# Down projection of a two-layer diffusion trunk: low parts of the operands moved from GpSimd to VectorE, raw granules three to five loaded ahead of the last store, and the post-norm sums taken one step later

## The chip, the cores and the metric

The kernel runs on one core of one Trainium2 chip. The metric is the device time of one execution in microseconds (us). The time before is the median of three runs. One further execution was recorded by the hardware profiler; every duration below comes from that one.

## The reference, cut to what matters

Two layers of a trunk over 1024 latent tokens, model width 1024, with 256 context tokens beside them. Each layer has a mixer and a gated feed-forward block; the change is in the last product of that block.

```python
def conv_ffn(h, w_up, conv_w, conv_b, w_down):
    u = h @ w_up
    u = lax.conv_general_dilated(u, ...) + conv_b      # width 3, over positions
    a, g = jnp.split(u, 2, axis=-1)
    return (jax.nn.silu(g) * a) @ w_down               # D_FF = 2816 -> 1024

x = x + g2 * rms_norm(conv_ffn(h_lat, ...), norm_post_ffn[l])
if with_ctx_out:                                       # layer 0 only
    ctx = ctx + g2c * rms_norm(conv_ffn(h_ctx, ...), norm_post_ffn[l])
```

All of it is in 32-bit floats, and the output is the latent stream after the second layer.

## The kernel before, in words

**The arithmetic.** TensorE multiplies the type called fp32r. To keep 32-bit accuracy each operand is split in two tiles: a high part (`d_Ah`, `d_Bh`; a cast on ScalarE, L1442) and a low part (`d_Al`, `d_Bl`; raw minus high, L1443, on VectorE or GpSimd, whichever `lo_engine` names). Each product is three matmuls: high by high, high by low of B, low of A by high.

**The down projection** (`ffn_down`) is a Strassen-like product with seven partial products, taken in the order P1, P5, P2, P3, P6, P4, P7. The contraction is cut in six *granules* per product (the sixth is half as wide), numbered 0 to 41 through the seven products (P1 is 0 to 5, P3 18 to 23, P6 24 to 29, P4 30 to 35, P7 36 to 41). A full granule is 24 matmuls of 128x128 by 512 columns. In P7 the last three granules are worked together, row block by row block, so that the four accumulators end one after the other. In layer 0 the context tokens follow as 22 more granules (42 to 63) of 12 matmuls each; layer 1 has none. A is the activation, read back from the DRAM tensor `actd`; B is the weight `w_down`. S and T (`d_s`, `d_t`) are kept sums of blocks, made by VectorE at L1447.

**Order.** In this stretch the instructions of TensorE, ScalarE, VectorE, GpSimd and, from the last step of the up projection on, of SyncE's queue stand in the order in which the program writes them. Each engine works strictly in that order. At step g the loop issues the products of granule g, then `prepare(g + 2)`: the splits (`prep`) of the granule two ahead (five ahead in the context part) and the loads that come after it, then whatever `todo` holds for that step. Operand tiles rotate over three places (six in the context part), so the splits of granule g wait until TensorE has finished granule g - 3. Raw tiles of B rotate over three buffers `w_raw`, those of A over four places `x_B22..`; `first_raws` names other places for the first few granules, tiles of the up projection that are no longer read.

**The start.** `ffn_down` is a generator that the last step of the up projection advances by `next(down, None)`: first the loads of granule 0, then its splits with the loads of 1 and 2, then the splits of 1 and 2. The store of the last activation tile to `actd` (L1262) waits for that step's last VectorE product. The loads of granules 3 and 4 follow it on SyncE's queue. The main loop then calls `loads(4)` once more, so granule 4 is loaded a second time, and `prep(4)` reads that second copy.

**Around the products.** `todo` holds the sums into `y` (L1569), squares on ScalarE (L1566), `scale` (L305, L110 on VectorE, then a power on GpSimd, L111), and `leave`: two scalings (L1591), two additions (L1569) on VectorE and a store issued from GpSimd's queue (L1595, L1597). Keys 0 to 3 are the latent rows whose sums end early; 4 to 7 end in P7; 8 and 9 are the context rows.

Of the kernel before, what the change touches and what calls it, by code (L numbers as in the profile page):

```python
# [50 lines left out]
class Trunk:  # L51
# [1136 lines left out]
    def ffn_up(self, l, src, ctx, x_src, x_dst, hp, pp, tp, es):  # L1188


        nc, a = self.nc, self.a
        raws, W, S, st = {}, {}, {}, {}
# [6 lines left out]
        def part(j, name):  # L1199
            if name[0] == "S":  # L1200
                return S[j, name]
            return raws[j, int(name[1]) - 1][:, 512 * (int(name[2]) - 1):512 * int(name[2])]

        def total(j, name, x, op, y):
            if j < FK:
                t = S[j, name] = sp.tile([P, 512], F32, name="w_s", bufs=3)
                nc.gpsimd.tensor_tensor(out=t, in0=part(j, x), in1=part(j, y), op=op)
# [9 lines left out]
        def product(ps, ws, x, start, stop):  # L1217

            jobs = [(W[w], k) for w in ws for k in range(4)]
            for i, ((wh, wl), k) in enumerate(jobs):  # L1220
                h, lo = wh[:, k * P:(k + 1) * P], wl[:, k * P:(k + 1) * P]
                xhk, xlk = X[x][i]
                self.mm(ps, h, xhk, start and i == 0, False)
                self.mm(ps, h, xlk, False, False)
                self.mm(ps, lo, xhk, False, stop and i == len(jobs) - 1)
# [50 lines left out]
        with self.in_order(*self.compute), ExitStack() as loads:  # L1276
# [4 lines left out]
            early = [lambda: split(0, "A11"), lambda: split(0, "A12")] + [lambda: split(0, "A21")] * ctx + [lambda: split(0, "A22")]  # L1281
# [24 lines left out]
            down = iter(())  # L1306
            for j in range(FK):
                n = j + 1
                if n == FK:
                    loads.enter_context(self.in_order(mybir.EngineType.SP))  # L1310
                    down = self.ffn_down(l, ctx, x_src, x_dst, hp, sp, pp, tp)
# [48 lines left out]
                if j == 0:  # L1360
                    next(sums)
                product(V[:, :512], ("A22",), "T4", True, True)
                total(n, "S3", "A11", OP.subtract, "A21")
                split(n, "S3")
                total(n, "S4", "A12", OP.subtract, "S2")
# [20 lines left out]
    def ffn_down(self, l, ctx, x_src, x_dst, hp, sp, pp, tp, beside=None):  # L1386
# [5 lines left out]
        nc, a = self.nc, self.a  # L1392
# [3 lines left out]
        NG = (H + 1) // 2  # L1396
        width = lambda c: min(2, H - 2 * c)

        def tile(pool, tag, name, n=1024, dtype=F32, bufs=1):
            return pool.tile([P, n], dtype, name=name, tag=tag, bufs=bufs)  # L1400
# [2 lines left out]
        s_home = [(hp, "x_T3" + x) for x in ("0h", "0l", "1h", "1l")] + [(hp, "x_T11l"), (self.wp, "w_A11l")]  # L1403
        t_home = [(hp, "n_t22")] * 2 + [(hp, "x_T1" + x) for x in ("0h", "0l", "1h")] + [(self.wp, "w_A11h")]

        first_raws = {(1, "A"): "x_T30h", (2, "A"): "x_T30l", (2, "B"): "x_T31h", (3, "A"): "x_T31l"}
        S, T, raws, opnd, count = {}, {}, {}, {}, {"A": 0, "B": 0}

        def load(dst, view, n):
# [29 lines left out]
        def split(side, slot, src, n, lo_engine):  # L1439
            tags = more[slot] if slot in more else [homes[slot % 3] + ("0" if side == "A" else "1") + x for x in "hl"]  # L1440
            hi, lo = (tile(hp, t, "d_" + side + x, dtype=F32R) for t, x in zip(tags, "hl"))
            nc.scalar.copy(hi[:, :n], src[:, :n])  # L1442
            lo_engine.tensor_tensor(out=lo[:, :n], in0=src[:, :n], in1=hi[:, :n].bitcast(F32), op=OP.subtract)  # L1443
            return hi, lo
# [35 lines left out]
        def prep(g):  # L1480
            if g >= NS + NC:
                return
            if g >= NS:
                k = g - NS
                opnd[g, "B"] = split("B", g, raws.pop((g, "B")), 1024, nc.gpsimd if k % 2 else nc.vector)
                if k % 4 == 0:
                    opnd[g, "A"] = split("A", k // 4, raws.pop((g, "A")), 256 * min(4, FK - k), nc.vector)
                return
            p, c = order[g // NG], g % NG
            n = 512 * width(c)  # L1490
            ra, rb = raws.pop((g, "A"), None), raws.pop((g, "B"), None)
            if p == "P7":
                total(T[c], rb, OP.subtract, T[c], n)
            elif p == "P4":
                total(rb, rb, OP.subtract, T[c], n)
            early = g < 3
            sides = (("A", S[c] if p in ("P5", "P6", "P7") else ra, nc.gpsimd if early else nc.vector),
                     ("B", T[c] if p in ("P5", "P6", "P7") else rb, nc.gpsimd if early or p in ("P3", "P4", "P7") else nc.vector))

            for side, src, engine in sides[::-1] if p in ("P3", "P5") else sides:  # L1500
                if side == "A" and p == "P5":
                    total(S[c], S[c], OP.add, ra, n)
                elif side == "A" and p == "P3":
                    total(ra, ra, OP.subtract, S[c], n)
                opnd[g, side] = split(side, g, src, n, engine)
            if p == "P1":
                after = lambda: total(T[c], T[c], OP.subtract, rb, n)
                if early:
                    return after
                after()  # L1510
            elif p == "P2":
                total(S[c], S[c], OP.subtract, raws.pop((g, "A2")), n)
            elif p == "P3":
                total(T[c], rb, OP.subtract, T[c], n)
            elif p == "P4":
                total(S[c], raws.pop((g, "A2")), OP.subtract, S[c], n)
# [45 lines left out]
        def at(g, f):  # L1562
            todo.setdefault(g, []).append(f)

        def square(src, ms, h):
            nc.scalar.activation(junk, src, AF.Square, scale=1.0 / 32.0, accum_out=ms[:, h:h + 1])  # L1566
# [18 lines left out]
        def scale(key, ms):  # L1585
            st["r", key] = self.y_rstd(ms)
# [15 lines left out]
        loads(1)  # L1602
        loads(2)
        yield
        after.append(prep(1))
        yield
        after.append(prep(2))
# [14 lines left out]
        y1b = [tile(p, "w_" + t, "y", 512) for p, t in ((self.wp, "A22h"), (self.wp, "A22l"), (sp, "S3h"), (sp, "S3l"))]  # L1622
        y2 = [tile(hp, "x_T4" + x, "y") for x in ("0h", "0l", "1h", "1l")]
        ms1, ms2 = ([self.small.tile([P, 2], F32, name=f"y_ms{j}", bufs=4) for _ in range(4)] for j in range(2))
        for i in range(4):
            at(NG + 1 + i, lambda i=i: nc.scalar.copy(p1[i], X[i]))
            at(2 * NG + 1 + i, lambda i=i: add(y2[i][:, 512:], Y[i], p1[i]))
            at(3 * NG + 1 + i, lambda i=i: (nc.scalar.copy(y1a[i], X[i]), square(X[i], ms1[i], 0)))
            at(4 * NG + 1 + i, lambda i=i: add(y1b[i], Y[i], p1[i]))
            at(5 * NG + 1 + i, lambda i=i: add(y1b[i], X[i], y1b[i]))  # L1630
            at(5 * NG + 2 + i, lambda i=i: (square(y1b[i], ms1[i], 1), scale(i, ms1[i])))
            at(6 * NG + 1 + i // 2, lambda i=i: add(y2[i][:, :512], Y[i], p1[i]))
        for i, (g, g1) in enumerate(((25, 33), (26, 35), (36, 38), (37, 39))):
            at(g, lambda i=i: fetch_x(i, i * P))
            at(g1, lambda i=i: leave(i, (y1a[i], y1b[i]), 0, i * P))
        r2 = lambda i: SEQ // 2 + i * P
# [11 lines left out]
        for i in range(5):  # L1648
            g = 6 * NG + (8 if ctx else 4) + gap * i
# [5 lines left out]
                at(g, lambda i=i - 1: leave(4 + i, halves(y2[i]), 0, r2(i), y2[i]))  # L1655
        for i in range(2 if ctx else 0):
            at(NS + NC - 4, lambda i=i: fetch_x(8 + i, SEQ + i * P))
        loads(3)
        loads(4)
        for kind in range(len(gates)):  # L1660
            for h in range(2):
                nc.sync.dma_start(gates[kind][h], self.gated[l, 1, kind][512 * h:512 * h + 512].partition_broadcast(P))
# [494 lines left out]
```

## Time and profile before

| what | value |
|---|---|
| median of three runs | 3511.76 us (3502.54 to 3518.81) |
| the profiled execution, its own time | 3511.39 us |
| its span in the profile | 3509.6 us (1.8 us lie around it) |
| TensorE busy | 3160.5 us, 90% of the span |
| VectorE busy | 2078.7 us, 59% |
| GpSimd busy | 1639.8 us, 47% |
| ScalarE busy | 1486.1 us, 42% |
| down projection of layer 0, first to last matmul | 1728.4 to 2032.8 us |
| down projection of layer 1, first to last matmul | 3257.9 to 3491.1 us |

The shares are means over stages of very different kinds. A matmul's recorded length overlaps that of its neighbours, so TensorE reads as fully busy whenever matmuls follow each other without a gap; what a stage loses is seen by counting its matmuls over its length.

### The profile page before, as it was taken

Reading aid. Unit: us, or ns where it says so; the run is one execution under the profiler, and the core shown is the slowest. Engines: PE = TensorE matmul, PEld = TensorE weight load, DVE = VectorE, ACT = ScalarE, POOL = GpSimd, SP = SyncE. Lnnn points to the kernel's source line nnn. Section 1 sums busy time; section 2 is a strip of 40 time slices with the busy share of each in tenths; the row PEclk is TensorE's granted clock in tenths of the full one; section 3 lists DMA queues with packets and bytes.
Section 4 is the critical chain, followed back from the end, with each engine's and each line's share of the span. In section 5 each row is a group of like instructions: output and inputs, shape, how many; then the busy total and the mean of one; then the engine's idle time right before and its main releaser. Section 6 shows DMA issues by size and latency. Waiting matters only on the chain. (4 is left out here: it accounts for less than half of the span.)

```text
span 3509.6 us, 49014 instructions
## 1 busy us (share of the span) xinstructions
PE 3160.5 (90%) x18364; PEld 2577.2 (73%) x18364; DVE 2078.7 (59%) x3366; ACT 1486.1 (42%) x2619; POOL 1639.8 (47%) x1174
## 2 busy tenths in 40 slices
PE   5989998779997899999999859999998689999997
PEld 2767676568885688888777638789986468888785
DVE  3525666557775744444578752477775564545678
ACT  3223222266664533333334441466674343434332
POOL 1300111187773566666413410577771167777124
PEclk7999999879998899999999979999998799999998
DMA  6533433321113122121466642222215412222755
GB/s 227 164 118 107 136 110 118 104 72 49 43 47 116 39 78 71 67 70 67 145 237 221 228 149 102 88 62 59 69 44 180 138 60 78 85 79 84 264 180 197
DMA packets 204845, 399.26 MB, mean 114 GB/s; under 512 B 24112, under 2 KB 86064, under 8 KB 204608
## 3 DMA queue, kind: packets, MB, share of 16 engines
q1 hardware_dynamic: 198432, 374.64, 32.2%
q0 software_dynamic: 6176, 21.50, 1.6%
q8 instruction: 144, 2.36, 0.3%
q14 instruction: 93, 0.76, 0.1%
HBM read 322.11 MB, written 74.34 MB: 113 GB/s over the span
## 5 line engine op out<-in xcount | busy, mean ns | idle before, releaser
L111 POOL TENSOR_TENSOR rs_r<-rs_e,mhalf 128x1 f32<-128x1 f32 (+3 forms) x106 | 79.6, 751 | 673.8 <-DVE rs_e L110 662.4
L103 PE MATMUL d_ps<-d_Bl,d_Ah 128*128 128x512 f32 x704 | 283.0, 402 | 19.0 <-POOL d_Bl L1443 15.2
L103 PE MATMUL d_ps<-d_Bh,d_Ah 128*128 128x512 f32 x704 | 281.9, 400 | 12.3 <-ACT d_Bh L1442 11.6
L103 PE MATMUL g_ps<-xh,w_hi 128*128 128x512 f32 (+1 forms) x704 | 279.5, 397 | 5.6 <-ACT w_hi L533 4.4
L103 PE MATMUL d_ps<-d_Bh,d_Al 128*128 128x512 f32 x704 | 281.1, 399 | 1.7 <-DVE d_Al L1443 1.7
L896 POOL TENSOR_SCALAR a_p<-a_p,rl 128x1280 f32<-128x1280 f32 (+1 forms) x80 | 240.4, 3010 | 73.4 <-DVE rl L895 65.3
L1857 POOL TENSOR_SCALAR c_p<-c_p,rl 128x640 f32<-128x640 f32 (+1 forms) x128 | 231.2, 1808 | 84.8 <-DVE rl L1856 59.8
L103 PE MATMUL g_ps<-xh,w_lo 128*128 128x512 f32 (+1 forms) x704 | 259.7, 369 | 4.7 <-POOL w_lo L1763 3.5
L103 PE MATMUL g_ps<-xl,w_hi 128*128 128x512 f32 (+1 forms) x704 | 259.8, 369 | 0.0
L1443 POOL TENSOR_TENSOR d_Bl<-d_rawB,d_Bh 128x1024 fp32r<-128x1024 f32 (+1 forms) x41 | 113.7, 2776 | 304.8 <-ACT d_Bh L1442 298.4
L1228 DVE TENSOR_TENSOR f_u<-u_v,f_p 128x512 f32<-128x512 f32 x88 | 60.5, 688 | 196.0 <-PE u_v L103 196.0
L103 PEld LDWEIGHTS d_ps<-d_Bl,d_Ah 128*128 128x128 f32 x704 | 136.0, 193 | 53.5 <-POOL d_Bl L1443 19.7
L918 DVE TENSOR_TENSOR a_pl<-a_pt,a_ph 128x512 fp32r<-128x512 f32 (+1 forms) x200 | 118.8, 603 | 89.3 <-ACT a_ph L917 88.8
L103 PEld LDWEIGHTS d_ps<-d_Bh,d_Ah 128*128 128x128 f32 x704 | 136.4, 194 | 45.7 <-ACT d_Bh L1442 14.9
L103 PEld LDWEIGHTS g_ps<-xh,w_hi 128*128 128x128 f32 x704 | 135.9, 193 | 45.4 <-issue 27.5
L1214 POOL TENSOR_TENSOR w_S4l<-w_s,w_S4h 128x512 fp32r<-128x512 f32 x44 | 57.2, 1301 | 237.4 <-ACT w_S4h L1213 237.4
L103 PEld LDWEIGHTS d_ps<-d_Bh,d_Al 128*128 128x128 f32 x704 | 136.3, 194 | 31.4 <-DVE d_Al L1443 2.9
L103 PEld LDWEIGHTS g_ps<-xh,w_lo 128*128 128x128 f32 x704 | 135.5, 192 | 29.4 <-POOL w_lo L1763 4.3
L103 PE MATMUL g_ps<-w_hi,xh 128*128 128x512 f32 (+1 forms) x400 | 153.7, 385 | 1.1 <-ACT w_hi L467 1.1
L917 ACT CAST a_ph<-a_pt 128x512 fp32r<-128x512 f32 (+1 forms) x200 | 102.9, 519 | 122.0 <-PE a_pt L916 122.0
L103 PE MATMUL g_ps<-w_lo,xh 128*128 128x512 f32 (+1 forms) x400 | 151.5, 379 | 0.8 <-DVE w_lo L468 0.8
L103 PE MATMUL g_ps<-w_hi,xl 128*128 128x512 f32 (+1 forms) x400 | 151.1, 378 | 0.2 <-DVE xl L268 0.2
(458 smaller groups left out, 9874.0 us busy)
## 6 DMA issues: line engine op xcount, KB each, us to landing
m_raw<-in_w_mod SPq DMA_DIRECT2D x96, 512.0 KB
w_raw<-in_w_up SPq DMA_DIRECT2D x88, 512.0 KB
d_rawA<-actd SPq DMA_DIRECT2D x77, 512.0 KB
d_rawB<-in_w_down SPq DMA_DIRECT2D x74, 512.0 KB
actd<-f_t SPq DMA_DIRECT2D x22, 640.0 KB
d_t<-in_w_down SPq DMA_DIRECT2D x22, 512.0 KB
actd<-f_t SPq DMA_DIRECT2D x22, 512.0 KB
d_s<-actd SPq DMA_DIRECT2D x20, 512.0 KB
```

The lines of the kernel that those rows point to most:

```text
L103: return self.nc.tensor.matmul(out, lhsT, rhs, start=start, stop=stop, skip_group_check=True, **k)
L111: nc.gpsimd.tensor_tensor(out=r[:p, :n], in0=e[:p, :n], in1=self.mhalf[:p, :n], op=OP.pow)
L896: nc.gpsimd.tensor_scalar(Pt[:, :nk], Pt[:, :nk], rl, None, op0=OP.mult)
L917: nc.scalar.copy(ph[:, j:j + n], pt[:, :n])
L918: nc.vector.tensor_tensor(out=pl[:, j:j + n], in0=pt[:, :n], in1=ph[:, j:j + n].bitcast(F32), op=OP.subtract)
L1214: nc.gpsimd.tensor_tensor(out=lo, in0=part(j, name), in1=hi.bitcast(F32), op=OP.subtract)
L1228: nc.vector.tensor_tensor(out=out, in0=x, in1=y, op=OP.add)
L1443: lo_engine.tensor_tensor(out=lo[:, :n], in0=src[:, :n], in1=hi[:, :n].bitcast(F32), op=OP.subtract)
L1857: nc.gpsimd.tensor_scalar(Pt[:, :n], Pt[:, :n], rl, None, op0=OP.mult)
```

## The change

Four edits. The step of the up projection advances the generator once more, and the loads of granules 3 and 4 move to that place, ahead of the last store. Raw tiles 3B, 4A, 4B and 5A get places of their own among the operand tiles `x_T4..` of the up projection, which are dead after its product T4. The low part of B in P3, P4, P7 and in every second context granule goes from GpSimd to VectorE, so that GpSimd makes low parts for granules 0 to 2 alone. And `scale` for keys 0 to 3 comes one step after the square it reads, with key 0's `leave` one step later too.

```diff
                 product(V[:, :512], ("A22",), "T4", True, True)
+                next(down, None)
                 total(n, "S3", "A11", OP.subtract, "A21")
...
-        first_raws = {(1, "A"): "x_T30h", (2, "A"): "x_T30l", (2, "B"): "x_T31h", (3, "A"): "x_T31l"}
+        first_raws = {(1, "A"): "x_T30h", (2, "A"): "x_T30l", (2, "B"): "x_T31h", (3, "A"): "x_T31l",
+                      (3, "B"): "x_T40h", (4, "A"): "x_T40l", (4, "B"): "x_T41h", (5, "A"): "x_T41l"}
...
-                opnd[g, "B"] = split("B", g, raws.pop((g, "B")), 1024, nc.gpsimd if k % 2 else nc.vector)
+                opnd[g, "B"] = split("B", g, raws.pop((g, "B")), 1024, nc.vector)
...
-                     ("B", T[c] if p in ("P5", "P6", "P7") else rb, nc.gpsimd if early or p in ("P3", "P4", "P7") else nc.vector))
+                     ("B", T[c] if p in ("P5", "P6", "P7") else rb, nc.gpsimd if early else nc.vector))
...
         loads(1)
         loads(2)
+        yield
+        loads(3)
+        loads(4)
         yield
         after.append(prep(1))
...
-            at(5 * NG + 2 + i, lambda i=i: (square(y1b[i], ms1[i], 1), scale(i, ms1[i])))
+            at(5 * NG + 2 + i, lambda i=i: square(y1b[i], ms1[i], 1))
+            at(5 * NG + 3 + i, lambda i=i: scale(i, ms1[i]))
...
-        for i, (g, g1) in enumerate(((25, 33), (26, 35), (36, 38), (37, 39))):
+        for i, (g, g1) in enumerate(((25, 34), (26, 35), (36, 38), (37, 39))):
...
-        loads(3)
-        loads(4)
         for kind in range(len(gates)):
```

SyncE's queue in layer 0 at the end of the up projection, before (numbers tell tiles of one name apart; 15848 to 15852 are granule 2, `actd_79<-f_t0_15855` is the last store, 15953 to 15957 granule 3, 15959 to 15963 granule 4, first load):

```order
L1410 DMA d_rawB_15848<-in_w_down 128x2x512
L1410 DMA d_rawA_15850<-actd_79 128x2x512
L1410 DMA d_t_15852<-in_w_down 128x2x512
L1262 DMA actd_79<-f_t0_15855 128x1280
L1410 DMA d_rawB_15953<-in_w_down 128x2x512
L1410 DMA d_rawA_15955<-actd_79 128x2x512
L1410 DMA d_t_15957<-in_w_down 128x2x512
L1410 DMA d_rawB_15959<-in_w_down 128x2x512
L1410 DMA d_rawA_15961<-actd_79 128x2x512
L1410 DMA d_t_15963<-in_w_down 128x2x512
L1662 DMA gate0_15925<-gated_75 128x512
```

and in the changed kernel:

```order
L1412 DMA d_rawB_15848<-in_w_down 128x2x512
L1412 DMA d_rawA_15850<-actd_79 128x2x512
L1412 DMA d_t_15852<-in_w_down 128x2x512
L1412 DMA d_rawB_15874<-in_w_down 128x2x512
L1412 DMA d_rawA_15876<-actd_79 128x2x512
L1412 DMA d_t_15878<-in_w_down 128x2x512
L1412 DMA d_rawB_15880<-in_w_down 128x2x512
L1412 DMA d_rawA_15882<-actd_79 128x2x512
L1412 DMA d_t_15884<-in_w_down 128x2x512
L1262 DMA actd_79<-f_t0_15855 128x1280
L1666 DMA gate0_15937<-gated_75 128x512
L1666 DMA gate0_15938<-gated_75 128x512
```

The six transfers of granules 3 and 4 stood behind the store and stand ahead of it now. The second load of granule 4 stands after the four `gate` loads in both.

VectorE in layer 0 around the turn from P4 to P7, before (the half granule 35 with its sums, then key 0's `leave`):

```order
L305 TENSOR_TENSOR yms<-y_ms_15945 128x1
L110 TENSOR_SCALAR rs_e<-yms 128x1
L1569 TENSOR_TENSOR y<-d_ps,y 128x512
L1447 TENSOR_TENSOR d_rawB<-d_rawB,d_t 128x512
L1443 TENSOR_TENSOR d_Al<-d_rawA,d_Ah 128x512
L1447 TENSOR_TENSOR d_s<-d_rawA,d_s 128x512
L305 TENSOR_TENSOR yms<-y_ms_15946 128x1
L110 TENSOR_SCALAR rs_e<-yms 128x1
L1569 TENSOR_TENSOR y<-d_ps,y 128x512
L1591 SCALAR_TENSOR_TENSOR y<-y,rs_r,gate_15925 128x512
L1591 SCALAR_TENSOR_TENSOR y<-y,rs_r,gate_15926 128x512
L1569 TENSOR_TENSOR y<-y,y_x 128x512 x2
```

and in the changed kernel (granule 35, then granule 36, the first of P7):

```order
L1449 TENSOR_TENSOR d_rawB<-d_rawB,d_t 128x512
L1445 TENSOR_TENSOR d_Al<-d_rawA,d_Ah 128x512
L1445 TENSOR_TENSOR d_Bl<-d_rawB,d_Bh 128x512
L1449 TENSOR_TENSOR d_s<-d_rawA,d_s 128x512
L305 TENSOR_TENSOR yms<-y_ms_15957 128x1
L110 TENSOR_SCALAR rs_e<-yms 128x1
L1571 TENSOR_TENSOR y<-d_ps,y 128x512
L1449 TENSOR_TENSOR d_t<-d_rawB,d_t 128x1024
L1445 TENSOR_TENSOR d_Al<-d_s,d_Ah 128x1024
L1445 TENSOR_TENSOR d_Bl<-d_t,d_Bh 128x1024
L305 TENSOR_TENSOR yms<-y_ms_15958 128x1
L110 TENSOR_SCALAR rs_e<-yms 128x1
```

Each granule has a `d_Bl` more on VectorE; the first `yms` stands behind granule 35's splits instead of ahead of them, and granule 36 comes ahead of key 0's `leave` instead of behind it.

GpSimd in layer 0 from P4's last granule on, before:

```order
L111 TENSOR_TENSOR rs_r<-rs_e,mhalf 128x1
L1443 TENSOR_TENSOR d_Bl<-d_rawB,d_Bh 128x512
L111 TENSOR_TENSOR rs_r<-rs_e,mhalf 128x1
L1595 DMA x2d<-y 128x512 x2
L1443 TENSOR_TENSOR d_Bl<-d_t,d_Bh 128x1024
L111 TENSOR_TENSOR rs_r<-rs_e,mhalf 128x1
L1443 TENSOR_TENSOR d_Bl<-d_t,d_Bh 128x1024
```

and in the changed kernel:

```order
L111 TENSOR_TENSOR rs_r<-rs_e,mhalf 128x1 x2
L1597 DMA x2d<-y 128x512 x2
L111 TENSOR_TENSOR rs_r<-rs_e,mhalf 128x1
L1597 DMA x2d<-y 128x512 x2
L111 TENSOR_TENSOR rs_r<-rs_e,mhalf 128x1
```

Only the powers and the stores are left there. TensorE's and ScalarE's order is the same in both kernels.

## Rows read from the trace of the kernel before

**Rows 1.** The stretches of layer 0's down projection, matmuls and weight loads that touch `d_ps` (and others that touch it): P1; P5 and P2; P3; P7; the context granules. Columns: stretch, length, then busy time and number of instructions for PE, PEld, DVE, ACT, then the granted TensorE clock, the DMA share and GB/s.

```profile
1728.40:1768.70 40.30, 34.39 (x132) 26.82 (x132) 0.00 (x0) 0.00 (x0) 0.92 0.81 293
1768.70:1828.50 59.80, 59.80 (x265) 49.51 (x265) 2.73 (x4) 2.31 (x4) 1.00 0.68 227
1828.50:1859.90 31.40, 30.59 (x134) 24.63 (x133) 0.00 (x0) 4.69 (x12) 1.00 0.36 128
1919.90:1962.60 42.70, 35.35 (x133) 26.99 (x132) 3.23 (x5) 0.00 (x0) 0.88 0.56 188
1962.60:2032.80 70.20, 64.17 (x264) 51.63 (x264) 5.50 (x9) 0.69 (x2) 0.95 0.73 252
```

**Rows 2.** The same for layer 1: P1; P3; P7.

```profile
3257.90:3297.10 39.20, 34.34 (x132) 26.97 (x133) 0.00 (x0) 0.00 (x0) 0.91 0.81 291
3356.90:3388.20 31.30, 30.49 (x133) 24.55 (x133) 0.00 (x0) 4.68 (x12) 1.00 0.39 130
3448.20:3491.10 42.90, 35.63 (x133) 27.27 (x132) 5.90 (x10) 0.00 (x0) 0.88 0.52 175
```

**Rows 3.** The longest of TensorE's waits in layer 0's down projection: engine and line, what it waited for, total us, times, longest.

```profile
PE d_ps L103 <- POOL d_Bl L1443: 10.3, 6, 2.9
```

**Rows 4.** Time line of ScalarE, then of VectorE, at P1's granules 3 and 4 in layer 0: start, length, instruction, count, and in brackets the idle time before it with what ended that.

```profile
1744.23 1.05 ACT L1442 CAST d_Ah<-d_rawA 128x1024 fp32r<-128x1024 f32 x1 [9.84 <-DMA d_rawA<-actd]
1755.62 1.04 ACT L1442 CAST d_Ah<-d_rawA 128x1024 fp32r<-128x1024 f32 x1 [9.40 <-DMA d_rawA<-actd]
...
1737.20 5.68 DVE L1447 TENSOR_TENSOR d_t<-d_t,d_rawB 128x1024 f32<-128x1024 f32 x3
1745.31 1.23 DVE L1443 TENSOR_TENSOR d_Al<-d_rawA,d_Ah 128x1024 fp32r<-128x1024 f32 x1 [2.43 <-ACT d_Ah L1442]
1746.45 1.22 DVE L1443 TENSOR_TENSOR d_Bl<-d_rawB,d_Bh 128x1024 fp32r<-128x1024 f32 x1
```

**Rows 5.** Time line of SyncE's queue in layer 0 from the last load of granule 2 on: the issue, its length, and the transfer.

```profile
1722.13 0.46 SPq L1410 DMA_DIRECT2D d_t<-in_w_down  x1
1737.34 0.34 SPq L1262 DMA_DIRECT2D actd<-f_t  x1
1737.78 0.38 SPq L1410 DMA_DIRECT2D d_rawB<-in_w_down  x1
...
1742.23 2.24 SPq L1662 DMA_DIRECT2D gate<-gated  x4
...
1746.86 0.37 SPq L1410 DMA_DIRECT2D d_rawA<-actd  x1
```

**Rows 6.** All engines by stretch around that store, layer 0 and (last row) layer 1. Columns as in rows 1, with POOL after ACT.

```profile
1723.00:1731.00 8.00, 6.39 (x29) 4.96 (x28) 5.26 (x6) 3.96 (x4) 2.59 (x2) 1.00 0.75 258
1731.00:1738.00 7.00, 7.00 (x33) 5.79 (x32) 5.40 (x4) 3.38 (x4) 6.68 (x3) 1.00 0.00 0
1738.00:1760.00 22.00, 16.10 (x58) 11.83 (x57) 11.68 (x9) 5.76 (x7) 1.53 (x1) 0.90 1.03 369
...
3259.50:3266.50 7.00, 7.00 (x33) 5.79 (x32) 5.25 (x6) 4.05 (x4) 6.90 (x4) 1.00 0.00 1
```

**Rows 7.** Layer 0's P4 (30 us of it), same columns; then VectorE's time line in P4 and at key 0's `leave`; between them one instruction of GpSimd.

```profile
1889.90:1919.90 30.00, 30.00 (x133) 24.59 (x131) 29.68 (x27) 10.85 (x16) 16.82 (x9) 1.00 0.86 303
...
1890.43 3.18 POOL L1443 TENSOR_TENSOR d_Bl<-d_rawB,d_Bh 128x1024 fp32r<-128x1024 f32 x1 [4.16 <-ACT d_Bh L1442]
...
1891.28 3.42 DVE L1447 TENSOR_TENSOR d_rawB<-d_rawB,d_t 128x1024 f32<-128x1024 f32 x1
1894.62 1.21 DVE L1443 TENSOR_TENSOR d_Al<-d_rawA,d_Ah 128x1024 fp32r<-128x1024 f32 x1
...
1896.89 3.42 DVE L1447 TENSOR_TENSOR d_rawB<-d_rawB,d_t 128x1024 f32<-128x1024 f32 x1
...
1908.11 2.34 DVE L305 TENSOR_TENSOR yms<-y_ms 128x1 f32<-128x1 f32 x1
1914.91 1.41 DVE L1591 SCALAR_TENSOR_TENSOR y<-y,rs_r,gate 128x512 f32<-128x512 f32 x2
1917.44 1.22 DVE L1447 TENSOR_TENSOR d_t<-d_rawB,d_t 128x1024 f32<-128x1024 f32 x1
```

**Rows 8.** TensorE's time line at the stalls of layer 0's P7.

```profile
1922.36 0.50 PE L103 MATMUL d_ps<-d_Bl,d_Ah 128*128 128x512 f32 x1 [1.94 <-POOL d_Bl L1443]
1948.27 0.79 PE L103 MATMUL d_ps<-d_Bh,d_Ah 128*128 128x512 f32 x1 [2.37 <-ACT d_Bh L1442]
```

**Rows 9.** The context granules of layer 0: TensorE at a stall, then GpSimd's time line around it.

```profile
1997.03 0.50 PE L103 MATMUL d_ps<-d_Bl,d_Ah 128*128 128x512 f32 x1 [2.95 <-POOL d_Bl L1443]
...
1993.47 0.57 POOL L1597 DMA_DIRECT2D x2d<-y  x1 [3.38 <-DVE y L1569]
1994.07 6.21 POOL L1443 TENSOR_TENSOR d_Bl<-d_rawB,d_Bh 128x1024 fp32r<-128x1024 f32 x2
```

**Rows 10.** From layer 0's down projection to the norm of layer 1: SyncE's queue, VectorE's last additions of key 7, ScalarE at a norm tile.

```profile
2018.00 5.47 SPq L1579 DMA_DIRECT2D y_x<-x1d  x2
2023.56 42.63 SPq L280 DMA_DIRECT2D n_x<-x2d  x97
...
2021.82 1.29 DVE L1569 TENSOR_TENSOR y<-y,y_x 128x512 f32<-128x512 f32 x2
...
2073.20 1.06 ACT L252 ACTIVATE junk<-n_x 128x1024 bf16<-128x1024 f32 x1 [4.21 <-DMA n_x<-x2d]
```

## The prediction

> **What bounds the kernel now.** The page's busy shares show TensorE at 90%, so I look for what it loses in the two down projections, the only place that the change touches. I read the stretches of its matmuls first [rows 1, 2]. From P5 through P2 it runs 264 matmuls in 59.8 us at a granted clock of 1.00: 0.2265 us each, 5.44 us for a granule of 24. At that pace the 132 matmuls of P1, of P3 with its neighbours' edge, or of P7 would take 29.9 us, and the 264 of the context 59.8. What is over is loss: in layer 0, P1 40.3 - 29.9 = 10.4, P3 1.5, P7 12.8, context 10.4; in layer 1, P1 9.3, P3 1.4, P7 13.0. That is 58.8 us, the most that the change can give back at TensorE. Part of it is clock: the granted clock is 0.92 in P1 and 0.88 in P7, so after a stall some matmuls ran at 1.2 GHz and not 2.4.
>
> Then the causes. In P1, ScalarE stands idle 9.84 and 9.40 us for a load of A [rows 4]. The store to `actd` is issued at 1737.34, 15 us after the last load of granule 2, and the loads of granule 3 come behind it [rows 5]; for the 7 us before it the DMA engines move nothing, after it they are full at 369 GB/s [rows 6]. In P7 and the context the largest wait is for GpSimd's low part of B, 10.3 us in six times [rows 3, 8, 9]. In P4 VectorE is busy 29.68 of 30.00 us, but not with work: at 1891.28 one L1447 takes 3.42 us while GpSimd's `d_Bl` runs from 1890.43 to 1893.61, while the next VectorE operation of the same size, at 1894.62, takes 1.21 [rows 7]. A VectorE operation that meets one of GpSimd's waits for its end.
>
> **The loads.** Six transfers of 128x1024 floats, 3.1 MB, move ahead of the store. From 1723 to 1731 the DMA engines run at 258 GB/s, 111 below their rate when full, which leaves 0.9 MB; from 1731 to 1738 they leave 2.6 MB [rows 6]. So the transfers fit and should land by about 1738. The store loses nothing: what holds it is VectorE's product. Granule 3 is due when TensorE has done three granules, 1728.4 + 16.3 = 1744.7. The three L1447 ahead of it on VectorE end at 1742.9 [rows 4]; `d_Al` and `d_Bl` at 1.14 each (1745.31 to 1746.45) end at 1745.2. A loss of 0.5 us remains. Granule 4 is read from its second load, which still stands behind store and gates: 0.66 MB, 1.05 MB and its own B and A, 1.05 MB, are 2.75 MB, or 7.5 us at 369 GB/s from 1737.3. With 2 us to arrive (an allowance of mine) and two casts of 1.05 it is ready at 1749, and TensorE comes to it at 1750.6. So 9.9 us come back in layer 0 and 8.8 in layer 1, where the same 7 us without DMA stand [rows 6]. Bounds: if the second load is 5 us later than that, 5 us less in each layer; if everything is in time, 0.5 more. The new places of the raw tiles cost nothing: the operands there are last read by T4, and `y` is written there only in P2, some 50 us after granule 5 has been read. If an old reader lingered, the loads would wait at the head of SyncE's queue, with the store behind them.
>
> **P3, P4 and P7.** GpSimd loses 18 low parts in each layer (15 full ones, like the one at 1890.43 of 3.18 us, and three of half width) and VectorE gains them at 1.14 [rows 4]. Per granule of P3 and P4 VectorE then has four operations, 4.6 us, where today's three take 5.61 (1891.28 to 1896.89 [rows 7]); TensorE takes 5.44. So P3's 2.9 us vanish.
>
> For the turn to P7 I follow VectorE's queue, from the moment when TensorE starts granule 34 and so frees the place of granule 36. The cast of A ends at 1.1; two low parts 3.4; key 1's sums and one addition 0.8, to 4.2; key 0's `leave` 2.53 (1914.91 to 1917.44), to 6.7. Granule 37: three operations and a sum, 3.6, to 10.3; `leave` of key 1, to 12.9. Granule 38, to 16.5. Granule 39 and two additions of 0.6, to 21.1; granule 40 the same, to 25.7; `leave` of key 2, to 28.2; granule 41's half-wide difference, to 28.8, and ScalarE's cast of it, 0.6, to 29.4. TensorE meanwhile needs 5.44 + 2.72 + 3 x 5.44 = 24.5 to the start of the last three granules, and comes to granule 41 after 12 matmuls more, at 27.2. So the stalls at P7's first and third granule go, and one remains: 2.2 us, 0.5 for the low part behind it, and, as behind the stall of 2.37 today, where the first matmul takes 0.79 [rows 8], some eight matmuls at the lower clock, 1.6. I leave 4.4 us in each layer: gains of 8.4 and 8.6. Bounds: nothing remains (12.8 and 13.0), or the stall stays as large as today, about 7.
>
> The later `scale` is a part of this queue. Its `yms`, one column, took 2.34 us at 1908.11 behind GpSimd [rows 7]; by itself it costs nothing, since key 0's result is needed only a step later. With ScalarE late, VectorE would wait in front of granule 36 instead; that is at most the 2.3 again.
>
> **The context granules and the step to layer 1.** At 1993.47 GpSimd's queue comes free of a store that waited 3.38 us for VectorE; the low part behind it is what TensorE waits 2.95 for [rows 9]. With the low parts on VectorE nothing but stores and powers is left to be held up there. But TensorE's end is not what counts here. SyncE's queue is held from 2018.00 to 2023.56 until key 7's `leave` frees a tile (its additions end at 2023.1); then it issues 97 loads of `n_x` without a break, 0.44 us each, and ScalarE still waits 4.21 us for one at 2073.20 [rows 10]. So layer 0 is worth what that `leave` moves. Today it ends 60.5 us after the context begins [rows 1, 10]. In the changed kernel VectorE has ahead of it, or in it, 25 low parts (28.5), four pairs of sums (4.8), four `leave` (10.1) and four `scale` (1.2): 44.6 us. I add 5 for raw tiles that arrive late at the start (three buffers) and 2 for casts that stand behind ScalarE's squares, less 1 for the start ahead of TensorE: 51. Gain 9.3. Bounds: 44 without idle time, and 60 if VectorE meets each wait of today.
>
> **Sum.** 9.9 + 8.8 + 2.9 + 8.4 + 8.6 + 9.3 = 47.9 us. The profiled execution took 3511.4, so 3463.5; it lies 0.4 below the median of the runs shown, so 3464.
>
> **Rivals.** *Half of it.* The second load of granule 4 comes 5 us late in both layers and P7's stall stays at 7: 10 + 5 less, 3479. For it: DMA is full from 1738 on, and my 2 us of arrival are an allowance; against: 1.6 us of slack on top.
>
> *VectorE becomes the bound, slower.* If L1447 in P4 stays at 3.42, 11 low parts in P4 and P7 cost 12.5 us in each layer and 11 in the context 12.5 more, 37.5; with P1's 18.7 given back, 3511.4 + 18.8 = 3530. It decides where L1447 stays above 5.44 - 3 x 1.14 = 2.0 us. Against it: each 3.42 us begins under a GpSimd low part, and those are gone. The Trainium skill (Perfetto Trace Analysis, Optimizing Scalar/DVE Operations) says that a saturated VectorE may be relieved by handing work to ScalarE or even GpSimd, though it adds that between VectorE and GpSimd this might not help, as they share a port. By its first half this change goes the wrong way, to the 3530; the row at 1891.28 speaks for the second.
>
> *Lost at the step to layer 1.* The 11 low parts come ahead of key 7's `leave` and nothing is saved: it ends 12.5 us later instead of 9.3 earlier, 3486. For it: VectorE's margin over TensorE in the context is thin, some 2 us by my queue; against: 44.6 us of work in 60.5.
>
> *The change does not bite.* Loads 3 and 4 push those of 1 and 2 back, and what P1 wins behind the store it loses ahead of it; little else comes: 3500 to 3515.
>
> **Chances.** Forecast 0.68, its own range 3453 to 3473; half of it 0.17; lost at the step 0.08; slower 0.04; no bite 0.03. The range 3450 to 3487 takes in the first three and the upper bounds of the loads and of P7. A difference of 0.5%, 17.6 us, is about what a measurement of this kernel can tell from none: faster 0.92, same 0.04, slower 0.04.
>
> **What would show it.** Right: ScalarE's idle time for `actd` at granules 3 and 4 below 1 us; the DMA engines busy just before the store; L1447 in P4 at 1.2 us; TensorE without a wait for `d_Bl` at P7's start, but one of about 2 us for `d_Bh` at granule 41; the first `n_x` load some 51 us after the context begins. Wrong: L1447 still at 3.4, a wait for `d_Bl` <- DVE all through P4 and the context, or granule 4 waiting for its load.

## The result, and the profile after

The changed kernel takes 3468.45 us in the median of six runs (3463.36 to 3476.25), where the kernel before took 3511.66 in six runs beside it: a ratio of 0.9877, 95% interval 0.9857 to 0.9897, or 36 to 50 us less. Forecast were 3464 and a range of 3450 to 3487. The profiled execution, 3476.25, is the slowest of the six, 7.8 above the median, so its trace shows 35 of the 43 us that the medians show.

The page of the changed kernel: its span, and the busy time of each engine with its share of the span and its instructions.

```profile
span 3474.5 us, 48963 instructions
PE 3145.1 (91%) x18364; PEld 2571.1 (74%) x18364; DVE 2059.0 (59%) x3413; ACT 1486.7 (43%) x2619; POOL 1516.2 (44%) x1127
```

VectorE has the 47 operations more that GpSimd has fewer, and is busy 20 us less: the times in which its operations stood still beside GpSimd's, as in [rows 7], are gone. The stretches of both down projections follow, in the columns of [rows 1]: layer 0's P1, P3, P7 and context, then layer 1's P1 and P7.

```profile
1723.30:1755.60 32.30, 30.88 (x132) 24.54 (x132) 0.00 (x0) 0.00 (x0) 1.00 1.00 358
1815.50:1845.40 29.90, 29.90 (x134) 24.75 (x133) 0.00 (x0) 4.69 (x12) 1.00 0.44 146
1905.20:1940.90 35.70, 32.32 (x134) 25.68 (x132) 2.56 (x4) 0.00 (x0) 0.95 0.61 201
1940.90:2003.10 62.20, 61.10 (x264) 49.23 (x264) 5.52 (x9) 0.69 (x2) 1.00 0.79 281
3239.90:3270.10 30.20, 30.16 (x132) 24.68 (x133) 0.00 (x0) 0.00 (x0) 1.00 1.01 360
3419.70:3456.00 36.30, 33.26 (x133) 26.42 (x131) 5.27 (x9) 0.00 (x0) 0.91 0.55 184
```

Less 29.9 (59.8 for the context), what is over is 2.4, 0, 5.8, 2.4 and 0.3, 6.4 us, where [rows 1, 2] had 10.4, 1.5, 12.8, 10.4 and 9.3, 13.0. TensorE's longest waits in layer 0's down projection, against [rows 3]:

```profile
PE d_ps L103 <- ACT d_Bh L1444: 3.5, 2, 3.1
PE d_ps L103 <- DVE d_Bl L1445: 1.6, 3, 1.0
PE d_ps L103 <- DVE d_Al L1445: 0.6, 1, 0.6
```

GpSimd is gone from the list, and VectorE's low parts put 1.6 us there in place of 10.3. What stands ahead is granule 41's cast in P7. Next, the stretch ahead of the store and the one behind it (columns as in [rows 6]), and SyncE's queue with VectorE's time line at that place (columns as in [rows 4, 5]):

```profile
1726.00:1733.00 7.00, 7.00 (x32) 5.79 (x32) 5.49 (x4) 5.18 (x6) 6.70 (x3) 1.00 0.94 348
1733.00:1755.00 22.00, 20.60 (x89) 16.00 (x88) 16.97 (x16) 6.09 (x7) 1.45 (x1) 1.00 1.01 355
```

```profile
1719.99 0.78 SPq L1412 DMA_DIRECT2D d_rawB<-in_w_down  x1
1720.82 1.70 SPq L1412 DMA_DIRECT2D d_rawA<-actd  x1
1722.96 0.75 SPq L1412 DMA_DIRECT2D d_t<-in_w_down  x1
1732.25 0.34 SPq L1262 DMA_DIRECT2D actd<-f_t  x1
...
1732.11 5.68 DVE L1449 TENSOR_TENSOR d_t<-d_t,d_rawB 128x1024 f32<-128x1024 f32 x3
1737.72 1.21 DVE L1445 TENSOR_TENSOR d_Al<-d_rawA,d_Ah 128x1024 fp32r<-128x1024 f32 x1
```

Seven us in which nothing moved now carry 348 GB/s. The store stands 8.95 us behind P1's first matmul, as before (1737.34 - 1728.40 there): the loads ahead of it cost it nothing.

### The profile page after: what moved, and what is told of

Same layout as the page of the kernel before. It is cut to its first block, busy times and chain, and to the rows that moved or that the text cites. A ratio compares the mean times of both kernels' runs of the same rounds, so it can differ in the third digit from the quotient of the medians.

```text
span 3474.5 us, 48963 instructions
## 1 busy us (share of the span) xinstructions
PE 3145.1 (91%) x18364; PEld 2571.1 (74%) x18364; DVE 2059.0 (59%) x3413; ACT 1486.7 (43%) x2619; POOL 1516.2 (44%) x1127
## 5 line engine op out<-in xcount | busy, mean ns | idle before, releaser
L1228 DVE TENSOR_TENSOR f_u<-u_v,f_p 128x512 f32<-128x512 f32 x88 | 60.5, 688 | 196.0 <-PE u_v L103 196.0
L1881 DVE TENSOR_TENSOR c_pl<-c_pt,c_ph 128x256 fp32r<-128x256 f32 (+1 forms) x256 | 113.0, 470 | 50.3 <-ACT c_ph L1880 48.9
```

Source lines behind the costliest of these rows:

```text
L1228: nc.vector.tensor_tensor(out=out, in0=x, in1=y, op=OP.add)
L1881: nc.vector.tensor_tensor(out=vap(pl, o, dims), in0=pt[:, :cnt], in1=vap(ph, o, dims).bitcast(F32), op=OP.subtract)
```

## Experiments

Ratios are to the kernel before in the same study, with a 95% interval. Losses are those of TensorE, as above: the length of a stretch less 0.2265 us for each matmul.

| kernel | ratio | interval | P1 | P3 | P7 | context | P1, L1 | P7, L1 |
|---|---|---|---|---|---|---|---|---|
| before | 1 | | 10.4 | 1.5 | 12.8 | 10.4 | 9.3 | 13.0 |
| changed | 0.9877 | 0.9857-0.9897 | 2.4 | 0 | 5.8 | 2.4 | 0.3 | 6.4 |
| loads alone | 0.9958 | 0.9944-0.9972 | 1.6 | 1.4 | 14.0 | 11.1 | 0.7 | 13.6 |
| low parts alone | 0.9935 | 0.9923-0.9948 | 10.9 | 0 | 5.3 | 1.2 | 9.7 | 6.4 |
| old places | 0.9929 | 0.9916-0.9942 | 10.8 | 0 | 6.7 | 1.2 | 9.3 | 5.3 |
| half of context on GpSimd | 0.9905 | 0.9892-0.9919 | 1.7 | 0 | 6.5 | 10.8 | 0.4 | 3.9 |
| sums with squares | 0.9878 | 0.9864-0.9891 | 1.2 | 0 | 3.3 | 2.3 | 0.6 | 3.1 |
| granule 4 once | 0.9891 | 0.9877-0.9905 | 0.4 | 0 | 6.6 | 1.3 | 0.1 | 3.9 |
| key 2 later | 0.9872 | 0.9856-0.9887 | 1.2 | 0 | 1.6 | 1.8 | 0.6 | 1.4 |
| half the loads from ScalarE | 0.9889 | 0.9875-0.9903 | 1.9 | 0 | 5.7 | 1.6 | 0.7 | 3.9 |
| three edits | 0.9859 | 0.9844-0.9874 | 1.2 | 0 | 0.8 | 1.6 | 0.1 | 0.6 |
| one load a tile | 0.9795 | 0.9782-0.9809 | 1.2 | 0 | 4.1 | 1.2 | 0.3 | 3.9 |
| four edits | 0.9764 | 0.9748-0.9780 | 0.4 | 0 | 0.8 | 1.2 | 0 | 0.6 |

**The loads alone.** The kernel before with the new places and the early loads:

```diff
+                next(down, None)
...
+                      (3, "B"): "x_T40h", (4, "A"): "x_T40l", (4, "B"): "x_T41h", (5, "A"): "x_T41l"}
...
+        yield
+        loads(3)
+        loads(4)
...
-        loads(3)
-        loads(4)
```

> The kernel before with the loads alone: loads of granules 3 and 4 ahead of the store, granules 3 to 5 in the places of dead operands; low parts and sums stay as before. If the terms of my sum add up independently, P1 loses about 2 us in layer 0 and under 1 in layer 1 (10.4 and 9.3 before), while P3, P7 and the context lose what they did: 17 us less, 3494. L1447-type differences in P4 stay at 3.4 us. If the loads only matter because VectorE took the low parts (granule 4's place is freed late by GpSimd), P1 keeps half of its loss: 3503. If an earlier P1 is given back at the step to layer 1, where SyncE's queue sets the pace, only layer 1's 9 us remain: 3503 too, but then with P1 of layer 0 at 2 us.

3491.26 us, 10 to 20 below the kernel before. P1's loss falls to 1.6 and 0.7, all else stays within 1.2 us: the first theory. VectorE's time line in P4 is as it was. Of the two differences of a granule (`d_s` and `d_rawB`) the second is held by GpSimd's low part, whose row stands last:

```profile
1877.41 1.21 DVE L1449 TENSOR_TENSOR d_s<-d_rawA,d_s 128x1024 f32<-128x1024 f32 x1
1878.55 3.42 DVE L1449 TENSOR_TENSOR d_rawB<-d_rawB,d_t 128x1024 f32<-128x1024 f32 x1
1889.77 2.34 DVE L305 TENSOR_TENSOR yms<-y_ms 128x1 f32<-128x1 f32 x1
...
1877.70 3.17 POOL L1445 TENSOR_TENSOR d_Bl<-d_rawB,d_Bh 128x1024 fp32r<-128x1024 f32 x1 [2.43 <-issue]
```

**The low parts alone.** The kernel before with the low parts on VectorE and the sums a step later:

```diff
-                opnd[g, "B"] = split("B", g, raws.pop((g, "B")), 1024, nc.gpsimd if k % 2 else nc.vector)
+                opnd[g, "B"] = split("B", g, raws.pop((g, "B")), 1024, nc.vector)
...
-                     ("B", T[c] if p in ("P5", "P6", "P7") else rb, nc.gpsimd if early or p in ("P3", "P4", "P7") else nc.vector))
+                     ("B", T[c] if p in ("P5", "P6", "P7") else rb, nc.gpsimd if early else nc.vector))
...
-            at(5 * NG + 2 + i, lambda i=i: (square(y1b[i], ms1[i], 1), scale(i, ms1[i])))
+            at(5 * NG + 2 + i, lambda i=i: square(y1b[i], ms1[i], 1))
+            at(5 * NG + 3 + i, lambda i=i: scale(i, ms1[i]))
...
-        for i, (g, g1) in enumerate(((25, 33), (26, 35), (36, 38), (37, 39))):
+        for i, (g, g1) in enumerate(((25, 34), (26, 35), (36, 38), (37, 39))):
```

> The kernel before with the low parts of all but three granules on VectorE and the sums a step later; the loads stay where they were. If the terms add up: P1 still loses 10 and 9 us; P3's 2.9 go, P7 loses 5 to 6 in each layer in place of 13, the context some 2 in place of 10, of which the step to layer 1 keeps 1 to 6: 3488 to 3493. If VectorE were the bound, P4 and P7 would show a wait for its low parts and the time would be above 3511. In both cases the differences in P4 should take 1.2 us and not 3.4, if GpSimd's low parts were what held them.

3487.20 us, 18 to 27 below. P1 loses what it did, P3 nothing, P7 less than half of what it did. With no low part on GpSimd the same operations in P4:

```profile
1877.44 1.22 DVE L1447 TENSOR_TENSOR d_rawB<-d_rawB,d_t 128x1024 f32<-128x1024 f32 x1
1878.91 1.23 DVE L1443 TENSOR_TENSOR d_Al<-d_rawA,d_Ah 128x1024 fp32r<-128x1024 f32 x1 [0.26 <-ACT d_Ah L1442]
1880.06 1.22 DVE L1443 TENSOR_TENSOR d_Bl<-d_rawB,d_Bh 128x1024 fp32r<-128x1024 f32 x1
```

3.42 has become 1.22, which decides against the rival in which VectorE becomes the bound; it now stands idle here for a cast. The Trainium skill (SBUF — State Buffer, Who interferes with whom) states that an operation of VectorE with both inputs in SBUF contends with GpSimd's reads, and that whoever is later stands still until the other ends. The rows agree: in the run before this one the 3.42 us end at 1881.97, 1.1 us behind GpSimd's low part, and here, without one, the same operation takes 1.22. How much of this half comes from VectorE no longer being held, and how much from low parts that stood in GpSimd's own queue [rows 9], no run separates. The two halves add up: 14.7 and 22.8 us by the ratios, 37.5, where the whole gives 43 with an interval of 36 to 50.

**The old places.** The changed kernel without the four new places:

```diff
-                      (3, "B"): "x_T40h", (4, "A"): "x_T40l", (4, "B"): "x_T41h", (5, "A"): "x_T41l"}
```

> The changed kernel without the new places: the early loads of granules 3 to 5 go to the rings of raw tiles (three for B, four for A). If the places are what lets the loads run ahead: the load of granule 4's B waits at the head of SyncE's queue for granule 0's raw B, which VectorE reads last 5 to 6 us after the store could go, and the store, the gates and all later loads stand behind it: P1 loses 5 to 10 us more in each layer, 3478 to 3488. If the places matter nothing because a tile is free by then: 3468, P1 at 2 us and 0.3 us.

3484.51 us; P1 loses 10.8 and 9.3 again. SyncE's queue:

```profile
1718.59 0.95 SPq L1411 DMA_DIRECT2D d_t<-in_w_down  x1
1735.37 0.37 SPq L1411 DMA_DIRECT2D d_rawB<-in_w_down  x1
1735.84 0.41 SPq L1411 DMA_DIRECT2D d_rawA<-actd  x1
1736.30 0.46 SPq L1411 DMA_DIRECT2D d_t<-in_w_down  x1
1736.86 0.42 SPq L1262 DMA_DIRECT2D actd<-f_t  x1
```

Granule 3's loads do go early, and TensorE's wait for that granule is all but gone. Then the queue waits 15.8 us at its head for VectorE to be done with a raw tile, so granule 4's early loads leave only a moment ahead of the store, and the store goes 13.8 us behind P1's first matmul (1736.86 - 1723.1) and not 8.95; TensorE waits 7.22 us for granule 4. Both edits are needed together: the places cost nothing, and without them the early loads bring P1 nothing.

**Half of the context back on GpSimd.**

```diff
-                opnd[g, "B"] = split("B", g, raws.pop((g, "B")), 1024, nc.vector)
+                opnd[g, "B"] = split("B", g, raws.pop((g, "B")), 1024, nc.gpsimd if k % 2 else nc.vector)
```

> The changed kernel with every second low part of the context granules back on GpSimd. In the changed kernel the context loses 2 us at TensorE in place of 10, but the first load of the norm was issued only 6 us earlier, counted from the start of the context. If TensorE's loss counts: 8 us slower than the changed kernel, 3476. If key 7's last step counts, by which SyncE's queue goes on to the norm: 6 us slower, 3474. If the step to layer 1 gives it all back: within 2 us of the changed kernel, 3468 to 3470.

3476.84 us: 8.4 above the changed kernel by the medians of two studies, and their intervals overlap by a little. TensorE loses 10.8 in the context, and the first load of the norm is issued 61.3 us after the context's first matmul, against 54.9 in the changed kernel and 60.9 before. So the low parts of the context are worth 8.4 at TensorE and 6 at SyncE's queue; the medians don't separate these two, but they speak against nothing being kept. The traces speak for it: from the context's first matmul to the first matmul into `c_s`, in layer 1's attention, 279.9 us pass here, 278.4 in the changed kernel and 277.6 in the kernel before. So this stays open.

**Sums with the squares.** The changed kernel with the last edit undone:

```diff
-            at(5 * NG + 2 + i, lambda i=i: square(y1b[i], ms1[i], 1))
-            at(5 * NG + 3 + i, lambda i=i: scale(i, ms1[i]))
+            at(5 * NG + 2 + i, lambda i=i: (square(y1b[i], ms1[i], 1), scale(i, ms1[i])))
-        for i, (g, g1) in enumerate(((25, 34), (26, 35), (36, 38), (37, 39))):
+        for i, (g, g1) in enumerate(((25, 33), (26, 35), (36, 38), (37, 39))):
```

> The changed kernel with the post-norm sums again in the same step as the squares, and key 0's last step again at step 33. My theory prices this edit at nothing: one column on VectorE waits at most some 2 us for ScalarE's square, in P4, where VectorE has 0.9 us of slack in a granule of 5.44 and TensorE is two granules behind: 0 to 2 us in each layer, 3468 to 3472, and P7's first and third granule still without a stall. The rival: it is this edit that takes away the stalls at P7's start, since VectorE stands behind the square while granule 36 waits; then 4 to 5 us come back in each layer, 3477.

3467.16 us, no difference that can be measured; the rival falls. But P7 loses less without the edit, 3.3 and 3.1: the wait at granule 41 is 2.28 us where the changed kernel waits 3.06. The time line of the changed kernel tells why:

```profile
1898.13 1.23 DVE L1445 TENSOR_TENSOR d_Al<-d_s,d_Ah 128x1024 fp32r<-128x1024 f32 x1 [0.81 <-ACT d_Ah L1444]
1899.27 1.22 DVE L1445 TENSOR_TENSOR d_Bl<-d_t,d_Bh 128x1024 fp32r<-128x1024 f32 x1
1900.41 0.16 DVE L305 TENSOR_TENSOR yms<-y_ms 128x1 f32<-128x1 f32 x1
...
1900.67 0.68 DVE L1571 TENSOR_TENSOR y<-d_ps,y 128x512 f32<-128x512 f32 x1
1901.27 1.41 DVE L1593 SCALAR_TENSOR_TENSOR y<-y,rs_r,gate 128x512 f32<-128x512 f32 x2
```

VectorE is idle 0.81 us ahead of granule 36, and key 0's last step (1901.27) stands behind it. With it at step 33, in the trace of this run, it starts at 1896.61 and VectorE has no idle time ahead of granule 36's low part; that this is the whole 0.78 is argued from the equal size.

**Granule 4 once.** `ready, loaded = 3, 5` in place of `3, 4`.

> The changed kernel, with granule 4 loaded once: the main loop goes on with granule 5, so 1.05 MB less are moved in P1 of each layer. In the changed kernel ScalarE's cast of granule 4's A waits for its second load, and TensorE loses 2.4 us in P1 of layer 0, 0.3 in layer 1. If the second load is what is late: P1 of layer 0 below 0.5 us, 3466. If it is VectorE's differences of the first three granules, as for granule 3: P1 stays at 2.4 us, 3468.

P1 loses 0.4 and 0.1: the second load was what came late. In the changed kernel ScalarE waits for it:

```profile
1744.02 1.05 ACT L1444 CAST d_Ah<-d_rawA 128x1024 fp32r<-128x1024 f32 x1 [12.84 <-DMA d_rawA<-actd]
```

The time, 3472.81, is not to be told from that of the changed kernel.

**Key 2 later.** `(36, 39)` in place of `(36, 38)` in the list of steps.

> The changed kernel with key 2's last step (2.53 us on VectorE) a step later, behind the difference and the low part of granule 41. In the changed kernel TensorE waits 3.05 us for granule 41's B, then runs up to 12 matmuls at 0.43 us: 5.8 and 6.4 us in P7. If it is VectorE's queue that is late, as in my working: the wait falls to about 0.5 us, the low clock with it, P7 loses 1 us in each layer; 3463 if layer 0's part is given back at the step to layer 1, 3458 if it is kept. If the raw tile or ScalarE is late, P7 stays as it is: 3468.

The wait at granule 41 falls to 0.53 in both layers, P7's loss to 1.6 and 1.4: VectorE's queue it was. Here is TensorE in P7 of the changed kernel, and below it of this one:

```profile
1927.49 0.51 PE L103 MATMUL d_ps<-d_Bh,d_Ah 128*128 128x512 f32 x1 [3.06 <-ACT d_Bh L1444]
1928.21 0.51 PE L103 MATMUL d_ps<-d_Bl,d_Ah 128*128 128x512 f32 x1 [0.22 <-DVE d_Bl L1445]
...
1929.79 0.63 PE L103 MATMUL d_ps<-d_Bh,d_Ah 128*128 128x512 f32 x1
1930.21 0.63 PE L103 MATMUL d_ps<-d_Bl,d_Ah 128*128 128x512 f32 x1
```

```profile
1924.84 0.49 PE L103 MATMUL d_ps<-d_Bh,d_Ah 128*128 128x512 f32 x1 [0.53 <-ACT d_Bh L1444]
1925.56 0.50 PE L103 MATMUL d_ps<-d_Bl,d_Ah 128*128 128x512 f32 x1 [0.23 <-DVE d_Bl L1445]
```

The median, 3465.72, lies 2.7 below the changed kernel, within what the runs scatter, although TensorE loses 9 us less in P7. In layer 1 0.7 us come back at the end, since VectorE's last steps follow P7 by 19.2 us and not by 18.5; for layer 0 the next experiments looked at the step to layer 1.

**Half of the norm's loads from ScalarE, and three edits together.**

```diff
-                    for r, part in view(xt):
-                        self.nc.sync.dma_start(r, part)
+                    for q, (r, part) in enumerate(view(xt)):
+                        (self.nc.scalar if l and q % 2 else self.nc.sync).dma_start(r, part)
```

> The changed kernel, where every second of the 128 loads of x2d for layer 1's norm is issued by ScalarE and not by SyncE. In all kernels so far SyncE issues them in 53 to 56 us, 0.43 us each. If the rate of issue is what bounds the step to layer 1, SyncE's 64 take 28 us and the step becomes 15 to 25 us shorter: 3445 to 3455. If the landing of the transfers bounds it: no change, 3468. If ScalarE's issues delay its squares as much as SyncE is relieved: within 5 us, 3465 to 3470.

> Three edits on the changed kernel: the sums again in the step of the squares with key 0's last step at step 33, key 2's last step behind granule 41, and every second load of x2d for layer 1's norm from ScalarE. If the stall at granule 41 is VectorE's queue, these two steps out of its way leave P7 under 1 us in both layers, 5 to 11 us; with what the loads bring (15 to 25 us) 3435 to 3450. If P7's gain is lost again in layer 0 and the loads bring nothing: 3462.

With half of the loads from ScalarE 3471.65 us: nothing gained, and no test of the rate of issue either. ScalarE issues its eight for a tile, waits with the square for that tile, and only then goes on with the next eight:

```profile
2011.29 4.47 ACTq L280 DMA_DIRECT2D n_x<-x2d  x5
2016.94 1.06 ACT L252 ACTIVATE junk<-n_x 128x1024 bf16<-128x1024 f32 x1 [5.56 <-DMA n_x<-x2d]
2016.99 1.17 ACTq L280 DMA_DIRECT2D n_x<-x2d  x3
2018.21 2.65 ACTq L280 DMA_DIRECT2D n_x<-x2d  x5
2022.02 1.06 ACT L252 ACTIVATE junk<-n_x 128x1024 bf16<-128x1024 f32 x1 [3.92 <-DMA n_x<-x2d]
```

The three edits give 3459.61; P7 is down to 0.8 and 0.6, the norm as slow as ever.

**One load for a tile.** The 16 transfers of 32 KB become one of 512 KB:

```diff
-                    return lambda xt: [(xt[8 * r:8 * r + 8], x2v[g, r]) for r in range(16)]
+                    return lambda xt: [(xt, x2v[g])]
```

> The changed kernel, where a tile of layer 1's norm is loaded from x2d by one transfer of 512 KB and not by 16 of 32 KB: SyncE issues 8 and not 128. With half of the issues on ScalarE nothing was gained, but there each issue stood behind a square that waited for its own tile, so the rate of issue was not tested. If 0.43 us for each of 128 issues is what bounds the step to layer 1, some 30 of its 63 us from the first load to the first matmul of layer 1 go: 3435 to 3445. If landing or the norm's own chain (square, power, scaling, transposes) bounds it: under 8 us, 3460 to 3468.

3439.77 us, 29 below the changed kernel. SyncE's queue there, first in the changed kernel, then in this one:

```profile
1995.76 56.06 SPq L280 DMA_DIRECT2D n_x<-x2d  x128
2052.00 0.35 SPq L282 DMA_DIRECT2D n_x<-x2d  x1
```

```profile
1988.39 4.27 SPq L1581 DMA_DIRECT2D y_x<-x1d  x2
1998.64 3.16 SPq L280 DMA_DIRECT2D n_x<-x2d  x5
2010.48 10.89 SPq L120 DMA_DIRECT2D w_raw<-in_w_qkv  x4
2024.84 1.82 SPq L280 DMA_DIRECT2D n_x<-x2d  x3
```

The row of 56.06 us is not one run of issues. From one issue to the next 0.34 us pass in the median, not 0.43, and ahead of the sixth tile the queue waits until TensorE's transposes free one of the five `n_x` tiles. Of the changed kernel, that wait (total, times, longest) and ScalarE's square for the eighth tile:

```profile
SPq L280 <- PE n_pt L264: 6.5, 1, 6.5
...
2053.75 1.06 ACT L252 ACTIVATE junk<-n_x 128x1024 bf16<-128x1024 f32 x1 [4.25 <-DMA n_x<-x2d]
```

The eighth tile's last issue ends at 2051.82, 1.93 us ahead of that square. In five of the eight tiles the square follows the last issue of its tile by 1.92 to 1.97 us (1.93 to 2.03 in the kernel before), while the DMA engines are busy 0.36 of these 56 us. So the rate of issue bounded the step from layer 0 to layer 1, in the kernel before as in the changed one, and not the landing or the norm's own work.

**Four edits.** The sums with the squares, key 2 later, granule 4 once, one load for a tile.

> The changed kernel with four edits: the sums again in the step of the squares and key 0's last step at step 33, key 2's last step behind granule 41, granule 4 loaded once, one load for each tile of layer 1's norm. P1 and P7 at 1 us or less in both layers, some 12 us under the changed kernel where nothing is given back; with the norm's loads 30 more: 3425 to 3435. If SyncE's queue no longer bounds the step, TensorE's end of layer 0 does, and then the gains of layer 0 count in full.

3427.83 us (3424.01 to 3436.84), 0.9764 of the kernel before and 41 us below the changed one. In both down projections together TensorE loses 3 us, where it lost 59 before.

## Why the prediction was right, step by step

The sum was 47.9 us; the medians give 43.2, the profiled execution 35.1. (Two of its steps are off by 0.1 and 0.2 us: 2.2 + 0.5 + 1.6 is 4.3 and not 4.4, and 60.5 - 51 is 9.5 and not 9.3.) By terms, from the stretches above:

- **P1, 9.9 and 8.8 forecast, 8.0 and 9.0 measured.** The loads fit ahead of the store, the store was not held, the DMA engines are busy where they stood still, and granule 3 costs 0.2 us where 0.5 were allowed. Granule 4 I had ready 1.6 us ahead of TensorE. It came late: its cast of A, at 1744.02 in the changed kernel, waits for the second load, and TensorE waits 0.45 and 0.96 us. That lies inside the bound that I gave for it, and loading it once takes it away. But two of my signs went against me: ScalarE's idle time for `actd` at granule 4 is 12.84 us and not below 1, since it is done with granule 3 early, and granule 4 waiting for its load is a sign that I had named for being wrong. The places cost nothing, as forecast.
- **P3, 2.9 forecast and measured.** Differences take 1.22 us, the four operations of a granule of P4 4.75 (from 1877.11 to 1881.85, two second differences in a row).
- **P7, 8.4 and 8.6 forecast, 7.0 and 6.6 measured.** The stalls at its first and third granule are gone and the one at granule 41 stands, as the queue said. It was traced to 28.2 us for the end of key 2's last step and 29.4 for the cast; measured from granule 34's start at 1897.07 they are 28.9 and 30.4 (VectorE goes on at 1925.97, the cast ends at 1927.44). Each of granules 37 to 40 takes VectorE 0.1 to 0.2 us longer than I counted, as where its second low part waits for the cast (1904.93 to 1906.18, 1.25 us in place of 1.14). With TensorE there at 27.2, as forecast, the wait is 3.06 and not 2.2, and the low clock behind it covers nine and twelve matmuls in the two layers and not eight. A step that failed is the price of the later sums: "by itself it costs nothing" left out that key 0's last step goes a step later with them, out of 0.81 us of idle time; without that edit the wait is 2.28.
- **The context and the step to layer 1, 9.3 forecast, about 6 measured at the place that I named.** The first load of `n_x` was to be issued 51 us after the context begins, and came after 54.9 (1995.76 - 1940.9). VectorE's work was as counted, 44.4 us of those 54.9; its idle time was not, since I had 5 us for late raw tiles and 2 for casts and it took 10. I also read the loads of `n_x` as issued without a break at 0.44 us each; the row that I read hides a wait of 6.3 us for a free tile (2054.20 to 2060.47 in the kernel before), and the issues stand 0.34 us apart. In the profiled execution nothing of the term is left at the first matmul into `c_s` (278.4 us behind the start of the context, 277.6 before), as below.
- **The rivals.** VectorE did not become the bound. Half of it would have needed the second load 5 us late, and in layer 0 it was about two (granule 4's casts end at 1746.02, 22.7 us behind P1's first matmul, where 20.6 were forecast). Of the rival lost at the step to layer 1 the place was right and the mechanism not: VectorE's order brought the first load forward by 6 us, but behind it the changed kernel's trace gives back 6.8.

Of the 12.8 us between the sum and the profiled execution, P1 accounts for 1.7, P7 for 3.4 and the first load for 3. The trace after also has 5.1 us to its credit that the change did not make: layer 0's P1 began at 1723.3 and not at 1728.4, with the same work ahead of it (in the kernels of this study anywhere from 1719.0 to 1729.6). So some 10 us were lost behind the first load. From it to the first matmul into `c_s`, in layer 1's attention, 216.7 us passed before and 223.5 after; in the other traces with half of the context's low parts on GpSimd it was 218.3 and 218.5, in those with all of them on VectorE and the same loads 219.6 to 225.2. Of the 6.8 us, 2.9 are a slower run of issues (56.06 us for the 128 loads, 53.14 before), and some 2 the clock, as in the last section. The 3 us that are left arose between there and layer 1's P1 (1017.7 before, 1020.7 after), where no edit reaches, and where other kernels of the study took 1016.8 to 1021.2.

So the terms of P1, P3 and P7 are borne out, 33.5 us of 38.6. That of the context is not shown: the traces find nothing kept, the medians with half of it back on GpSimd some 8 us. That the medians of the changed kernel come as near to the sum as they do is in part luck: they gained 8 us more than the profiled execution, and no trace shows where.

## What to carry to other kernels

Where an engine's operation takes three times its usual time, look for what runs on the engine beside it: here moving work from GpSimd to a VectorE that seemed 99% busy made VectorE less busy, by 20 us over the whole execution. A load that is issued early must have a place that is free early, since it waits at the head of a queue with everything behind it. And before a term is counted at an engine's end, follow it to the queue that sets the next stage's pace: 128 small loads there were worth more, 29 us, than either half of this change.

## What the runs showed of the hardware that I had not expected

**The clock gives some of it back.** Behind TensorE's last long wait of the norm, 2.5 to 3.6 us for a tile in the nine kernels that issue all 128 loads from SyncE, the next 15 us ran at the full clock in the three traces with every second context low part on GpSimd (before, loads alone, half of the context back), and at 0.81 to 0.89 in the six with these on VectorE (changed, low parts alone, old places, sums with squares, granule 4 once, key 2 later). The rows of the kernel before, then of the changed one, in the columns of [rows 6]:

```profile
2101.83:2116.83 15.00, 15.00 (x70) 11.64 (x71) 6.91 (x19) 5.93 (x11) 0.00 (x0) 1.00 0.18 70
```

```profile
2077.26:2092.26 15.00, 15.00 (x61) 12.05 (x62) 6.59 (x18) 5.46 (x10) 0.00 (x0) 0.82 0.18 70
```

Nine matmuls fewer in the same time are 2 us that the context's gain lost again. What differs ahead of that wait is not settled; its length alone is not it, with 2.55 to 3.27 us in the three and 2.74 to 3.56 in the six.

**The same stall may cost twice.** In P7 a wait of 3.05 us was followed by six to thirteen slower matmuls, most of them at 0.43 us, the 1.2 GHz level, in some traces, and by none in others of the same code: layer 1's P7 lost 6.4 us in the changed kernel and 3.9 in that with granule 4 loaded once. After waits of 2.28 and 0.53 us none of them slowed (the 2.37 us of [rows 8], with other stalls shortly ahead of it, did slow some). So P7 lost 3.9 to 6.7 us with the same wait of 3.05, and 3.1 to 3.3 with 0.78 us less of it.
